# First group's shift and scale from row tiles of the conditioning weights, summed on DVE; tokens scaled on ACT

## Chip, cores, metric

One Trainium2 chip, one of its cores. The metric is the device time of one execution of the whole kernel in microseconds (us), as a median over runs. The engines are named as in the profile: PE is TensorE (PEld its weight loads), DVE is VectorE, ACT is ScalarE, POOL is GpSimd, SP is SyncE, which issues nearly all DMAs. MB are 10^6 bytes.

## The reference

One layer of a decoder trunk over 2048 tokens of width 1024 in float32. Only its beginning matters here: six vectors of 1024 values come from a conditioning vector c and a weight matrix, and the first two shift and scale the normalised tokens ahead of one wide projection.

```python
cond = jax.nn.silu(c)
mod = cond @ ada_w[l] + ada_b[l]                 # ada_w: 1024 x 6144
shift_m, scale_m, gate_m, shift_f, scale_f, gate_f = jnp.split(mod[:, None, :], N_MOD, axis=-1)
h = rms_norm(x, mix_norm_g[l]) * (1 + scale_m) + shift_m
proj = h @ w_in[l] + b_in[l]
...
x = x + gate_m * mixed
...
return rms_norm(x, final_norm_g)
```

Attention, a gated linear recurrence (HGRN2), an output projection and a gated feed-forward layer with a short convolution follow.

## The kernel before

Tokens are worked on in four groups of 512 (four blocks of 128 tokens). Channels stand in eight tiles of 128, index `k`. For each group the tokens are normalised, transposed with channels on the partitions, shifted and scaled, and split into a high part rounded to fp32r and a low part, the rest. Weights are split in the same way, and every product is three matmuls (high by high, high by low, low by high) that add up in one PSUM bank: `mm3`.

The first group has a stage of its own, in which everything is held in the written order on each engine (`pin(True, ...)` to `pin(False, ...)`, by `keep_in_program_order`); instructions that are not held are put into the engines' queues by the planner of the tile framework, the setup's mask tiles (`lvt`, `lev`) and other constants among them. The stage computes five projections of 128 columns (`first_cols`) for 512 tokens, with the loop over `k` outside, so that each of the eight steps needs shift and scale of 128 channels only: `first_mm(k, i)` is one `mm3` of step `k` into bank `ps0[i]`. That makes 8 x 5 x 3 = 120 matmuls of 128x512.

What a step needs, by name:

- `load_ada0(t)` loads one column tile of `ada_w`, all 1024 rows by 128 columns (0.5 MB, as 128 partitions x 8 rows of 512 B). Tiles 8 to 15 give the scale of channel tile `k`, tiles 0 to 7 its shift. Twelve buffers. SP issues them in written order with the loads of x, of the projection weights (`load_w0(kh)`, five loads for each half of the channels) and of later constants (`rB`).
- `first_mod(k)` multiplies a tile by `cond` (one instruction of 128x1024) and adds its eight parts in halves (512, 256, 128 columns). The scale tile is always DVE's; the shift tile is TensorE's for k = 0, DVE's for k = 1 and GpSimd's for k = 2 to 7 (`SHIFT`).
- `first_ab(k)` sums over the partitions with matmuls of one column into `mod_ps`; its `end()` adds biases on ACT and leaves shift and scale in `abm`.
- `norm_x` squares a token block on ACT, DVE adds the two halves, GpSimd makes the reciprocal root; `scale_x` multiplies the tokens by it, on DVE.
- `turn_x(k)` transposes four blocks on TensorE into the one bank `tp`; `first_h(k)` applies `abm` on ACT (tile `hf_h`), rounds the high part on ACT (`hhi`), and DVE subtracts for the low part (`hlo`).
- `split_w0(kh, ...)` splits the five weight tiles of one half: high parts on ACT (`w0h`), low parts (`w0l`) on DVE, in the first half two of five on GpSimd.

Step `k` hands the work of step `k + 1` to the queues ahead of its own products, and the sums of step `k + 3`. Behind the stage follow the other projections, HGRN2 and attention of group 0, then the other groups; the remaining 32 column tiles of `ada_w` are summed there, by `mod_part`, and are not touched.

Of the kernel before, what the change touches and what calls it, by code (L numbers as in the profile page):

```python
# [8 lines left out]
F32 = mybir.dt.float32  # L9
# [3 lines left out]
AF = mybir.ActivationFunctionType  # L13
ALU = mybir.AluOpType
# [4 lines left out]
P = 128  # L19
D = 1024  # L20
KT = D // P
KH = KT // 2
# [31 lines left out]
def kernel(ctx, tc, x, c, ada_w, ada_b, mix_norm_g, w_in, b_in, attn_sinks, attn_out_g,  # L54
# [32 lines left out]
    def bank(name, tag):  # L87
        return psp.tile([P, 512], F32, tag=tag, bufs=BANKS[tag], name=name)
# [43 lines left out]
    def col(nm, i=0, n=1):  # L132
        o = names[nm] + i
        return cols[:, o:o + n]
# [1 line left out]
    modc = const.tile([P, 48], F32, name="modc")  # L136
    abm = const.tile([P, 4, KT], F32, name="abm")

    def mod_sums(eng, raw, ns, times=True):

        if times:
            eng.tensor_tensor(out=raw, in0=raw, in1=cond.unsqueeze(2).broadcast_to([P, KT, P]), op=ALU.mult)
        for n in ns:
            eng.tensor_tensor(out=raw[:, 0:n, :], in0=raw[:, 0:n, :], in1=raw[:, n:2 * n, :], op=ALU.add)

    def mod_col(ps, raw, n, by=None):
        for k in range(n):
            TE.matmul(ps, lhsT=raw[:, k, :], rhs=ones[:, 0:1] if by is None else by[:, k:k + 1], start=k == 0,
                      stop=k == n - 1)

    def mod_ab(slot, gname, shift0, scale0, k0, n):
        ks_ = slice(k0, k0 + n)
        V.scalar_tensor_tensor(out=abm[:, slot, ks_], in0=modc[:, scale0 + k0:scale0 + k0 + n], scalar=1.0,
# [76 lines left out]
    with ExitStack() as mx:  # L230
# [18 lines left out]
        V.tensor_tensor(out=cond, in0=psC[:, 0:KT], in1=cond, op=ALU.mult)  # L249


        xs, xi = [], [None]
        ada0 = {}

        def load_x(b):
            if b < BPG:
# [10 lines left out]
                SY.dma_start(out=hs[i], in_=x_v[b * P:(b + 1) * P, i * 512:(i + 1) * 512])  # L267
            return hs

        def load_ada0(t):  # L270
            ada0[t] = su.tile([P, KT, P], F32, tag="ada0", bufs=12, name=f"ada0_{t}")
            SY.dma_start(out=ada0[t], in_=ada_v[:, :, t * P:(t + 1) * P])

        xs.append(load_x(0))
        load_ada0(8)
        xs.append(load_x(1))
        load_ada0(0)
        xs.append(load_x(2))
        xs.append(load_x(3))
        psA = bank("rowsA", "tp")  # L280
        TE.transpose(psA[:, 0:nA], rA[0:nA, :], ident[0:nA, 0:nA])
        V.tensor_copy(out=cols[:, 0:nA], in_=psA[:, 0:nA])
# [4 lines left out]
        def norm_x(t, b):  # L287
            r = norm_rows(su if b < BPG else mt, t, f"x{b}", "ln", 3)
            if b < BPG:
                return r  # L290
            for half in t:
                V.tensor_scalar(out=half, in0=half, scalar1=r, scalar2=None, op0=ALU.mult)
# [89 lines left out]
        ps0 = [bank(f"ps0_{i}", t) for i, t in zip(range(len(first_cols)), ("mm", "mm", "mm", "hg", "hg", "at"))]  # L382
        mod_ps = bank("mod_ps", "at")
        tps = {}
        SHIFT = [TE, V, G, G, G, G, G, G]

        def first_mod(k):
            for t in (KT + k, k):
                if t not in ada0:
                    load_ada0(t)  # L390
            mod_sums(V, ada0[KT + k], (4, 2, 1))
            if SHIFT[k] is not TE:
                mod_sums(SHIFT[k], ada0[k], (4, 2))

        def first_ab(k):

            ps = mod_ps[:, 2 * k:2 * k + 2]
            mod_col(ps[:, 0:1], ada0[KT + k], 1)
            if SHIFT[k] is TE:
                mod_col(ps[:, 1:2], ada0[k], KT, cond)  # L400
            else:
                mod_col(ps[:, 1:2], ada0[k], 2)

            def end():
                S.activation(abm[:, 0, k:k + 1], ps[:, 0:1], AF.Identity, scale=col("mix_g", k), bias=abg[:, k:k + 1])
                S.activation(abm[:, 1, k:k + 1], ps[:, 1:2], AF.Identity, bias=col("ada_b", k))
            return end

        def turn_x(k):
            tps[k] = bank(f"tp0_{k}", "tp")  # L410
            for b in range(BPG):
                TE.transpose(tps[k][:, b * P:(b + 1) * P], xs[b][k // 4][:, k % 4 * P:(k % 4 + 1) * P], ident)

# [7 lines left out]

        def scale_x(b, r):
            for half in xs[b]:
                V.tensor_scalar(out=half, in0=half, scalar1=r, scalar2=None, op0=ALU.mult)

        r = norm_x(xs[0], 0)
        mod_sums(V, ada0[KT], (4,))
        scale_x(0, r)
        r = norm_x(xs[1], 1)
        mod_sums(V, ada0[KT], (2, 1), False)  # L430
        scale_x(1, r)
        load_w0(0)
        ab0 = first_ab(0)
        r = norm_x(xs[2], 2)
        scale_x(2, r)
        r = norm_x(xs[3], 3)
        ab0()
        scale_x(3, r)
        turn_x(0)
        split_w0(0, (V, G))  # L440
        first_h(0)
        first_mod(1)
        turn_x(1)
        first_mm(0, 0)
        first_mm(0, 1)
        if SHIFT[1] is TE:
            first_ab(1)()
        for i in range(2, len(first_cols)):
            first_mm(0, i)
        if SHIFT[1] is not TE:  # L450
            first_ab(1)()
        first_mod(2)
        first_h(1)
        first_mod(3)
        load_w0(1)
        for k in range(1, KT):
            pos = [0,0,0,0,0,0,0,0][k]
            for i in range(len(first_cols)):
                if i == pos and k + 1 < KT:
                    turn_x(k + 1)  # L460
                    first_ab(k + 1)()
                    first_h(k + 1)
                    if k + 3 < KT:
                        first_mod(k + 3)
                if k == 2 and i == 2:
                    split_w0(1, (V, V))
                first_mm(k, i)
            if k == 5:
# [1116 lines left out]
```

## Time and profile before

| | |
|---|---|
| time, median of 3 runs | 2443.85 us (2443.26 to 2449.54) |
| the profiled execution | 2448.34 us, its span 2446.3 us |
| mean granted TensorE clock | 0.975 of full |
| PE busy | 2294.8 us, 94% |
| DVE busy | 1912.5 us, 78% |
| ACT busy | 966.7 us, 40% |
| POOL busy | 931.7 us, 38% |
| end of the first group's five projections | last of 120 matmuls starts at 80.94 us |

The busy times are those of the whole span, and say little about one stage: the first 81 us are 3% of it. For a stage the profile is asked for stretches of time (busy time of each engine between two times), for the timeline (instructions in order of time, equal neighbours merged) and for the waits (which engine sat idle, and whose signal ended it). A matmul's printed duration overlaps its neighbour's; the distance between two starts is what one takes. Line L46 is the helper that issues every instruction, so instructions are told apart by their tiles.

### The profile page before, as it was taken

The numbers are of one execution on the slowest core, as the hardware profiler recorded it, in microseconds if no ns is written. First come the engines' busy times: TensorE is split into PE (matmuls) and PEld (weight loads), VectorE is DVE, ScalarE is ACT, GpSimd is POOL, SyncE is SP. The second block draws the span as 40 slices with busy tenths as digits, with TensorE's granted clock in tenths as the row PEclk, the third lists the DMA queues.
The fourth block names the chain that finished last, engine by engine and source line by source line (L and its number), as shares of the span: only waits on it lengthen the run. The fifth ranks groups of instructions, "written<-read, shape, count | busy, mean of one in ns | idle before, by whom it ended". The sixth has DMA issues, their size and how long they took to land. (4 is left out here: it accounts for less than half of the span.)

```text
span 2446.3 us, 31473 instructions
## 1 busy us (share of the span) xinstructions
PE 2294.8 (94%) x11521; PEld 1904.1 (78%) x11521; DVE 1912.5 (78%) x2737; ACT 966.7 (40%) x1658; POOL 931.7 (38%) x776
## 2 busy tenths in 40 slices
PE   5889898998999899999999999999999989998997
PEld 4877787887788787887888888778888768786775
DVE  8888768788867877378888888878878688777666
ACT  3336523723552363455333333433333343233322
POOL 6222212213122222032756666478888721110101
PEclk8999999999999999999999999999999989999999
DMA  8342323323231238475434433554555488887543
GB/s 216 91 121 91 91 69 105 95 70 112 79 95 53 86 113 267 157 248 155 146 97 144 151 117 114 191 176 156 163 153 166 138 267 248 215 209 239 182 171 124
DMA packets 335445, 359.74 MB, mean 147 GB/s; under 512 B 12405, under 2 KB 279371, under 8 KB 335291
## 3 DMA queue, kind: packets, MB, share of 16 engines
q1 hardware_dynamic: 320315, 301.36, 39.3%
q0 software_dynamic: 14976, 56.37, 8.5%
q8 instruction: 91, 1.49, 0.2%
q14 instruction: 63, 0.52, 0.1%
HBM read 250.19 MB, written 107.49 MB: 146 GB/s over the span
## 5 line engine op out<-in xcount | busy, mean ns | idle before, releaser
L46 DVE SCALAR_TENSOR_TENSOR cc<-ub,cols,cc 128x1024 f32<-128x1024 f32 x88 | 153.2, 1741 | 15.5 <-ACT cc L46 13.3
L46 PE MATMUL lv<-a_q,K 128*128 128x128 f32 (+2 forms) x768 | 80.5, 265 | 42.7 <-DVE K L46 38.2
L46 ACT ACTIVATE Th<-da 128x896 fp32r<-128x896 f32 x88 | 81.8, 945 | 92.6 <-PE ps_d L46 88.2
L46 PEld LDWEIGHTS lv<-a_q,K 128*128 128x128 f32 (+2 forms) x768 | 72.2, 177 | 55.6 <-DVE K L46 28.8
L46 POOL DMA_DIRECT2D x_d<-o x32 | 27.2, 858 | 218.6 <-DVE o L46 218.6
L46 DVE TENSOR_TENSOR o<-ps_d,u 128x512 f32<-128x512 f32 x72 | 49.5, 687 | 71.6 <-ACT u L46 34.8
L46 DVE TENSOR_TENSOR Tl<-da,Th 128x896 fp32r<-128x896 f32 x88 | 94.5, 1099 | 12.8 <-ACT Th L46 12.8
L46 POOL TENSOR_TENSOR s<-wu_0r,s 128x512 f32<-128x512 f32 x44 | 59.2, 1347 | 107.2 <-DVE ws_0l L46 14.6
L46 DVE TENSOR_TENSOR cc<-cc,v 128x1024 f32<-128x1024 f32 x44 | 64.2, 1459 | 43.5 <-ACT cc L46 43.4
L46 POOL MEMSET AT<- 128x512 f32 x16 | 8.5, 533 | 234.8 <-PE ho L46 211.8
L46 POOL TENSOR_TENSOR s<-wu_1r 128x512 f32<-128x512 f32 x44 | 70.0, 1590 | 70.7 <-DVE t_T4l L46 16.2
L46 POOL TENSOR_TENSOR wu_1r<-wu_0r,wu_1r 128x512 f32<-128x512 f32 x44 | 93.3, 2121 | 3.1
L46 ACT ACTIVATE cc<-cc 128x1024 f32<-128x1024 f32 x44 | 46.7, 1061 | 120.8 <-DVE cc L46 120.8
L46 POOL TENSOR_SCALAR rv_d<-ssd 128x1 f32<-128x1 f32 x16 | 14.8, 925 | 181.6 <-ACT dx L46 181.6
L46 POOL TENSOR_TENSOR pl<-raw,ph 128x512 fp32r<-128x512 f32 x32 | 44.3, 1388 | 99.3 <-ACT ph L46 83.6
L46 POOL TENSOR_TENSOR s<-s,wu_0r 128x512 f32<-128x512 f32 x44 | 73.6, 1672 | 0.0
L46 DVE TENSOR_TENSOR v<-ps_u,v 128x512 f32<-128x512 f32 x88 | 60.4, 686 | 15.2 <-PE ps_u L46 11.9
L46 DVE COPY_PREDICATED AT<-lev,lv 128x512 f32<-128x512 uint32 (+1 forms) x96 | 70.1, 731 | 2.4 <-PE lv L46 1.1
L46 ACT ACTIVATE cc<-ub,cols 128x1024 f32<-128x1024 f32 x44 | 54.6, 1240 | 25.9 <-DVE ub L46 25.9
L46 DVE TENSOR_TENSOR ada<-ada,cond 128x1024 f32<-128x1024 f32 (+1 forms) x37 | 52.3, 1414 | 14.3 <-DMA ada<-in_ada_w_dram 14.3
L46 DVE TENSOR_TENSOR a_q<-a_q,tot 128x256 f32<-128x256 f32 x96 | 52.1, 543 | 12.4 <-PE lv L46 11.1
L46 DVE TENSOR_TENSOR ada<-ada 128x512 f32<-128x512 f32 (+3 forms) x82 | 61.2, 747 | 0.9
(2114 smaller groups left out, 8562.9 us busy)
## 6 DMA issues: line engine op xcount, KB each, us to landing
da<-act_d SPq DMA_DIRECT2D x88, 448.0 KB, 8.0
wu_0r<-in_w_up_dram SPq DMA_DIRECT2D x44, 512.0 KB, 4.6
wu_1r<-in_w_up_dram SPq DMA_DIRECT2D x44, 512.0 KB, 4.3
act_d<-cc POOLq DMA_DIRECT2D x42, 512.0 KB, 4.1
ada<-in_ada_w_dram SPq DMA_DIRECT2D x40, 512.0 KB, 6.0
x_d<-o POOLq DMA_DIRECT2D x32, 512.0 KB, 7.9
act_d<-sm POOLq DMA_DIRECT2D x21, 768.0 KB, 4.2
x<-in_x_dram SPq DMA_DIRECT2D x26, 512.0 KB, 5.6
```

The lines of the kernel that those rows point to most:

```text
L46: ins = fn(*args, **kwargs)
```

## The change

Shift and scale of the first group are computed for half of the channels at a time (`half`, four channel tiles), not for one tile. `load_ada0(half, k)` loads a row tile: 128 rows of `ada_w`, 512 columns of shift and 512 of scale (0.5 MB, 128 partitions x 2 rows of 2 KB); there are ten buffers. `first_mod(half, k)` adds it, times its column of `cond`, to a running sum in one DVE instruction of 128x1024 (for k = 0 a multiplication alone). After eight of them `first_ab(half)` makes eight one-column matmuls and three small DVE operations. GpSimd makes no sums and no low parts of weights. `scale_x` is on ACT. All eight tiles of the first half are asked for among the loads of x, ahead of the projection weights; those of the second half behind the first weights, the last two of them behind the second weights. Transposes have a second bank in turn, the tag `at`, and are issued a step earlier. The sums of the second half stand in steps 0 to 2, `split_w0(1)` at the start of step 3 and `first_ab(1)` behind two of its five products.

```diff
--- before.py
+++ after.py
@@ -136,18 +136,6 @@
     modc = const.tile([P, 48], F32, name="modc")
     abm = const.tile([P, 4, KT], F32, name="abm")
 
-    def mod_sums(eng, raw, ns, times=True):
-
-        if times:
-            eng.tensor_tensor(out=raw, in0=raw, in1=cond.unsqueeze(2).broadcast_to([P, KT, P]), op=ALU.mult)
-        for n in ns:
-            eng.tensor_tensor(out=raw[:, 0:n, :], in0=raw[:, 0:n, :], in1=raw[:, n:2 * n, :], op=ALU.add)
-
-    def mod_col(ps, raw, n, by=None):
-        for k in range(n):
-            TE.matmul(ps, lhsT=raw[:, k, :], rhs=ones[:, 0:1] if by is None else by[:, k:k + 1], start=k == 0,
-                      stop=k == n - 1)
-
     def mod_ab(slot, gname, shift0, scale0, k0, n):
         ks_ = slice(k0, k0 + n)
         V.scalar_tensor_tensor(out=abm[:, slot, ks_], in0=modc[:, scale0 + k0:scale0 + k0 + n], scalar=1.0,
@@ -249,8 +237,9 @@
...
         xs, xi = [], [None]
-        ada0 = {}
+        ada0, ada_sum = {}, {}
 
         def load_x(b):
             if b < BPG:
@@ -267,16 +256,27 @@
                 SY.dma_start(out=hs[i], in_=x_v[b * P:(b + 1) * P, i * 512:(i + 1) * 512])
             return hs
 
-        def load_ada0(t):
-            ada0[t] = su.tile([P, KT, P], F32, tag="ada0", bufs=12, name=f"ada0_{t}")
-            SY.dma_start(out=ada0[t], in_=ada_v[:, :, t * P:(t + 1) * P])
+        def load_ada0(half, k):
+
+            r = ada0[half, k] = su.tile([P, 2, 512], F32, tag="ada0", bufs=10, name=f"ada0_{half}_{k}")
+            SY.dma_start(out=r, in_=ada_v[:, k, 0:2 * D].rearrange("p (s c) -> p s c", s=2)
+                         [:, :, half * 512:(half + 1) * 512])
+
+        def first_mod(half, k):
+            raw = ada0.pop((half, k))
+            if k == 0:
+                ada_sum[half] = su.tile([P, 2, 512], F32, tag="adas", bufs=2, name=f"adas_{half}")
+                V.tensor_scalar(out=ada_sum[half], in0=raw, scalar1=cond[:, 0:1], scalar2=None, op0=ALU.mult)
+            else:
+                V.scalar_tensor_tensor(out=ada_sum[half], in0=raw, scalar=cond[:, k:k + 1], in1=ada_sum[half],
+                                       op0=ALU.mult, op1=ALU.add)
 
         xs.append(load_x(0))
-        load_ada0(8)
         xs.append(load_x(1))
-        load_ada0(0)
-        xs.append(load_x(2))
-        xs.append(load_x(3))
+        for k in range(KT):
+            load_ada0(0, k)
+            if k in (1, 2):
+                xs.append(load_x(k + 1))
         psA = bank("rowsA", "tp")
         TE.transpose(psA[:, 0:nA], rA[0:nA, :], ident[0:nA, 0:nA])
         V.tensor_copy(out=cols[:, 0:nA], in_=psA[:, 0:nA])
@@ -382,32 +382,21 @@
         ps0 = [bank(f"ps0_{i}", t) for i, t in zip(range(len(first_cols)), ("mm", "mm", "mm", "hg", "hg", "at"))]
         mod_ps = bank("mod_ps", "at")
         tps = {}
-        SHIFT = [TE, V, G, G, G, G, G, G]
-
-        def first_mod(k):
-            for t in (KT + k, k):
-                if t not in ada0:
-                    load_ada0(t)
-            mod_sums(V, ada0[KT + k], (4, 2, 1))
-            if SHIFT[k] is not TE:
-                mod_sums(SHIFT[k], ada0[k], (4, 2))
-
-        def first_ab(k):
-
-            ps = mod_ps[:, 2 * k:2 * k + 2]
-            mod_col(ps[:, 0:1], ada0[KT + k], 1)
-            if SHIFT[k] is TE:
-                mod_col(ps[:, 1:2], ada0[k], KT, cond)
-            else:
-                mod_col(ps[:, 1:2], ada0[k], 2)
-
-            def end():
-                S.activation(abm[:, 0, k:k + 1], ps[:, 0:1], AF.Identity, scale=col("mix_g", k), bias=abg[:, k:k + 1])
-                S.activation(abm[:, 1, k:k + 1], ps[:, 1:2], AF.Identity, bias=col("ada_b", k))
-            return end
+
+        def first_ab(half):
+
+            ps = mod_ps[:, 8 * half:8 * half + 8]
+            for i in range(2):
+                for kk in range(KH):
+                    TE.matmul(ps[:, 4 * i + kk:4 * i + kk + 1], lhsT=ada_sum[half][:, i, kk * P:(kk + 1) * P],
+                              rhs=ones[:, 0:1], start=True, stop=True)
+            ks_ = slice(KH * half, KH * half + KH)
+            V.tensor_tensor(out=abm[:, 0, ks_], in0=ps[:, 4:8], in1=col("mix_g", KH * half, KH), op=ALU.mult)
+            V.tensor_tensor(out=abm[:, 0, ks_], in0=abm[:, 0, ks_], in1=abg[:, ks_], op=ALU.add)
+            V.tensor_tensor(out=abm[:, 1, ks_], in0=ps[:, 0:4], in1=col("ada_b", KH * half, KH), op=ALU.add)
 
         def turn_x(k):
-            tps[k] = bank(f"tp0_{k}", "tp")
+            tps[k] = bank(f"tp0_{k}", "at" if k % 2 else "tp")
             for b in range(BPG):
                 TE.transpose(tps[k][:, b * P:(b + 1) * P], xs[b][k // 4][:, k % 4 * P:(k % 4 + 1) * P], ident)
 
@@ -421,48 +410,43 @@
 
         def scale_x(b, r):
             for half in xs[b]:
-                V.tensor_scalar(out=half, in0=half, scalar1=r, scalar2=None, op0=ALU.mult)
-
-        r = norm_x(xs[0], 0)
-        mod_sums(V, ada0[KT], (4,))
-        scale_x(0, r)
-        r = norm_x(xs[1], 1)
-        mod_sums(V, ada0[KT], (2, 1), False)
-        scale_x(1, r)
+                S.activation(half, half, AF.Copy, scale=r)
+
+        r0 = norm_x(xs[0], 0)
+        r1 = norm_x(xs[1], 1)
+        scale_x(0, r0)
+        first_mod(0, 0)
+        first_mod(0, 1)
+        r2 = norm_x(xs[2], 2)
+        scale_x(1, r1)
+        first_mod(0, 2)
+        r3 = norm_x(xs[3], 3)
+        scale_x(2, r2)
+        scale_x(3, r3)
+        turn_x(0)
+        turn_x(1)
         load_w0(0)
-        ab0 = first_ab(0)
-        r = norm_x(xs[2], 2)
-        scale_x(2, r)
-        r = norm_x(xs[3], 3)
-        ab0()
-        scale_x(3, r)
-        turn_x(0)
-        split_w0(0, (V, G))
+        for k in range(3, KT):
+            first_mod(0, k)
+        for k in range(6):
+            load_ada0(1, k)
+        load_w0(1)
+        for k in range(6, KT):
+            load_ada0(1, k)
+        first_ab(0)
         first_h(0)
-        first_mod(1)
-        turn_x(1)
-        first_mm(0, 0)
-        first_mm(0, 1)
-        if SHIFT[1] is TE:
-            first_ab(1)()
-        for i in range(2, len(first_cols)):
-            first_mm(0, i)
-        if SHIFT[1] is not TE:
-            first_ab(1)()
-        first_mod(2)
-        first_h(1)
-        first_mod(3)
-        load_w0(1)
-        for k in range(1, KT):
-            pos = [0,0,0,0,0,0,0,0][k]
+        split_w0(0, (V, V))
+        for k in range(KT):
             for i in range(len(first_cols)):
-                if i == pos and k + 1 < KT:
-                    turn_x(k + 1)
-                    first_ab(k + 1)()
+                if k == 3 and i == 2:
+                    first_ab(1)
+                if k + 1 < KT and i == (2 if k == 3 else 0):
                     first_h(k + 1)
-                    if k + 3 < KT:
-                        first_mod(k + 3)
-                if k == 2 and i == 2:
+                    if k + 2 < KT:
+                        turn_x(k + 2)
+                if k < 3 and i in (1, 2, 3) and 3 * k + i < 9:
+                    first_mod(1, 3 * k + i - 1)
+                if k == 3 and i == 0:
                     split_w0(1, (V, V))
                 first_mm(k, i)
             if k == 5:
```

## Rows read from the trace of the kernel before

**Rows 1.** Stretches: us, engines' busy us (instructions), TensorE clock, DMA share, GB/s.

```profile
0.00:20.00 20.00, 6.22 (x26) 5.28 (x27) 12.00 (x38) 11.16 (x28) 7.89 (x18) 1.00 0.93 273
20.00:44.00 24.00, 9.46 (x30) 6.84 (x28) 23.86 (x31) 2.13 (x5) 16.87 (x12) 0.76 1.14 279
44.00:65.00 21.00, 19.16 (x82) 15.76 (x83) 20.69 (x22) 8.40 (x18) 13.33 (x8) 0.79 0.28 76
65.00:81.40 16.40, 16.34 (x81) 13.13 (x80) 12.35 (x26) 11.56 (x19) 0.69 (x2) 1.00 0.60 184
```

**Rows 2.** Timeline, TensorE: start us, us, line, operation, tiles, count [idle before <-releaser].

```profile
12.20 3.55 PE L46 MATMUL mod_ps<-cond,ada 128*128 128x1 f32 x16
...
24.24 0.79 PE L46 MATMUL ps<-hlo,w0h 128*128 128x512 f32 x1 [3.09 <-DVE hlo L46]
...
29.33 0.39 PE L46 MATMUL ps<-hlo,w0h 128*128 128x512 f32 x1
...
50.77 0.60 PE L46 MATMUL tp<-ident,x 128*128 128x128 f32 x4
...
54.09 0.39 PE L46 MATMUL ps<-hhi,w0h 128*128 128x512 f32 x1
54.32 0.40 PE L46 MATMUL ps<-hlo,w0h 128*128 128x512 f32 x1
...
57.92 0.83 PE L46 MATMUL mod_ps<-ones,ada 128*128 128x1 f32 x6 [1.83 <-DVE ada L46]
...
59.89 0.63 PE L46 MATMUL ps<-hhi,w0l 128*128 128x512 f32 x1
60.31 0.63 PE L46 MATMUL ps<-hhi,w0h 128*128 128x512 f32 x1
...
80.94 0.40 PE L46 MATMUL ps<-hhi,w0l 128*128 128x512 f32 x1
```

**Rows 3.** Waits until 82 us: who waited for whom, us, times, longest.

```profile
ACT abm L46 <- PE mod_ps L46: 38.1, 8, 16.9
```

**Rows 4.** Stretches of the ada tile alone: us, busy us of each engine, clock, DMA.

```profile
20.00:45.00 25.00, 2.48 (x11) 2.31 (x12) 13.04 (x12) 17.74 (x11) 0.75 1.10 268
...
60.00:81.40 21.40, 2.18 (x18) 2.25 (x18) 6.30 (x11) 0.00 (x0) 0.92 0.55 165
```

**Rows 5.** Timeline, DVE: start us, us, tiles, one addition of 128x512.

```profile
25.44 2.38 DVE L46 TENSOR_TENSOR ada<-ada 128x512 f32<-128x512 f32 x1
```

**Rows 6.** Tile hf_h until 90 us: count, ns min/median/max, first to last start.

```profile
L46 ACT ACTIVATE hf_h<-tp,abm x8: 772/778/783, 18.8 to 74.7; 128x512 f32<-128x512 f32 x8
L46 ACT ACTIVATE hhi<-hf_h x8: 630/632/633, 19.6 to 75.5; 128x512 fp32r<-128x512 f32 x8
L46 DVE TENSOR_TENSOR hlo<-hf_h,hhi x8: 678/683/694, 23.5 to 76.2; 128x512 fp32r<-128x512 f32 x8
```

**Rows 7.** Tile lvt, the setup's masks, until 90 us, same columns.

```profile
L46 DVE SCALAR_TENSOR_TENSOR lvt<-fx,up_s x5: 280/292/1980, 14.2 to 37.1; 128x128 f32<-128x128 f32 x5
```

**Rows 8.** Tile cc, a later stage of the kernel, same columns.

```profile
L46 DVE SCALAR_TENSOR_TENSOR cc<-ub,cols,cc x88: 1271/1694/2301, 1142.5 to 1977.9; 128x1024 f32<-128x1024 f32 x88
```

**Rows 9.** Stretches, DMA: us, TensorE clock, DMA share, GB/s.

```profile
0.00:5.00 5.00, 1.00 0.35 104
5.00:10.00 5.00, 1.00 1.09 333
10.00:12.00 2.00, 1.00 1.05 400
20.00:28.00 8.00, 1.00 1.21 291
64.00:66.00 2.00, 1.00 1.08 381
```

**Rows 10.** Timeline, ACT: the first square of the second token block.

```profile
9.50 0.63 ACT L46 ACTIVATE junk_x<-x 128x512 f32<-128x512 f32 x1 [2.20 <-DMA x<-in_x_dram]
```

**Rows 11.** Timeline, DVE: one small operation of eight columns.

```profile
4.22 0.16 DVE L46 SCALAR_TENSOR_TENSOR abg<-cols 128x8 f32<-128x8 f32 x1
```

## Prediction

> **What bounds the kernel now.** I read the stretches of the first 81 us before anything else, because the diff touches only the work up to the end of the first group's five projections. [rows 1] show a stage that is not held by TensorE: its 120 products need 120 x 0.234 = 28 us at the high clock, 2.4 GHz (spacing in [rows 2]: 54.09 to 54.32), yet the last one starts at 80.94. In 20 to 44 us DVE is busy 23.9 of 24 and GpSimd 16.9, in 44 to 65 DVE 20.7 of 21; only after 65, with GpSimd at 0.7, is TensorE busy throughout. DMA carries 279 GB/s until 44 us and then has almost nothing to do (76 GB/s). So DVE sets the pace from 20 to 65 us, beside a DMA stream for the first half of that time.
>
> The view of waits says for whom that matters: ACT waits 38.1 us in eight waits for the sums that give it shift and scale [rows 3]. The stretches of the ada tile alone show DVE's share: 13.0 us in 12 instructions while GpSimd does 17.7 us on its own ada tiles, and 6.3 us in 11 when GpSimd does none [rows 4]. One instruction shows the same: a 128x512 addition takes 2.38 us at 25.44 [rows 5]; the same shape with two inputs takes 0.68 where GpSimd is idle (the low part in [rows 6], its shortest). A 128x128 mask operation goes from 0.28 to 1.98 us [rows 7]. GpSimd's sums and DVE's hold each other up.
>
> **The change, part by part.**
>
> *Sums.* Removed: fifteen of the sixteen 0.5 MB column tiles with a multiplication and two or three additions each, six on GpSimd (the sixteenth is multiplied on TensorE). Added: sixteen row tiles, one 128x1024 instruction each on DVE. The shortest three-operand instruction of that shape takes 1.27 us [rows 8]; the longest there, 2.30, has GpSimd beside it, and there is no such neighbour now. I take 1.27, so 8 x 1.27 = 10.2 us per half, against the DVE-and-GpSimd work of [rows 4], 33 us of DVE alone over the stage.
>
> *DMA.* The bytes are the same, but rows of 512 B become rows of 2 KB. 512 B rows run at 291 GB/s (20 to 28 us), a stretch of 1 KB rows at 381 (64 to 66), and one that holds mostly 4 KB rows at 400 (10 to 12) [rows 9]. No row shows 2 KB alone, so the bounds are 291 and 400; I take 370, next to the 1 KB row. The Trainium skill (DMA: Bandwidth & Descriptors, section Where 436 GB/s comes from) puts the HBM side of one core at about 358 GB/s. By that the first half would land 0.5 us later; the 381 of the row speaks against a cap there, and the sum does without it.
>
> The order is changed too: x and all eight tiles of the first half come before the projection weights, the second half behind those. By 5 us 0.52 MB have arrived [rows 9]. x1 needed 1.6 MB, which the 333 GB/s of 5 to 10 us deliver at 8.3; ACT started on it at 9.50 [rows 10], so a tile is usable 1.2 to 1.3 us after its bytes by rate. The last tile of half 0 ends 6.34 MB: 5 + 5.82/0.37 = 20.7, usable 22.0. The first half of the weights (1.31 MB, 512 B rows still) is usable from about 23 to 26.5; ACT comes to it at 27, so its place behind the tiles costs nothing. The second half of ada and of the weights ends at 25.2 + 4.19/0.37 + 1.31/0.291 = 41.0, usable 42.2. Ten buffers stand for sixteen loads: load 11 waits for sum 1 (done about 11 us), load 16 for sum 6 (about 20), before SP reaches them. The small loads of later constants stay behind it on SP and are not needed until the seventh step.
>
> *First product.* Sum 7 of half 0 ends at 22.0 + 1.3 = 23.3. Eight 128x1 products: 16 took 3.55 us, soon after TensorE's start [rows 2], so 1.8; three small DVE operations 3 x 0.16 [rows 11]; ACT h 0.78, ACT high part 0.63 [rows 6], first weight split another 0.63; 27.7, with handovers 28.0. Before, products run from 24.24 [rows 2]: this later start is the price of the change. ACT scaling x instead of DVE: eight operations of at most 0.63, done by 20, under the arrival of the tiles. DVE's weight low parts (0.68 each, five, no longer shared with GpSimd) keep ahead of three products at 1.28.
>
> *Loop.* TensorE resumes at the low clock, 1.2 GHz (spacing 0.42, as from 59.89 to 60.31): from 24.24 it took until 29.33 for the spacing to halve [rows 2]. I count ten products of step 0 at 0.427 and five at 0.234: 5.4, to 33.4. Steps 1 and 2 are 15 x 0.234 + 0.6 for four transposes [rows 2] = 4.1 each, to 41.6, and two projections of step 3 to 43.0. DVE in that time: low parts and the second half's sums, the last of them after its tile, 42.2 + 1.3 = 43.5; here the DMA is late next, TensorE waits 0.5. Then column products 0.9 (high clock), but DVE has the five weight low parts of the second half ahead of the three small operations: 43.5 + 5 x 0.68 + 0.5 = 47.4, ACT h 48.2, high part 48.8, low part 49.5. TensorE has the rest of step 3 and four transposes until 47.2, so it waits 1.6 us plus 0.5 within step 4. Step 4 ends at 49.5 + 14 x 0.234 = 52.8, step 5 with transposes 56.9, step 6 60.4, step 7 with the constants' transpose 64.2. Before, the last product starts at 80.94 and ends the stage at 81.2. Saved: 17.0.
>
> *Corrections.* (a) The masks: sixteen DVE operations of the setup that are not held in written order stand inside this stage, 0.28 us apiece [rows 7], 4 us in all. If all lay between the last sum and the first product they cost 4, if all lay before, 0. DVE needs some 12 of the first 23 us, so I take 1. (b) A TensorE wait of 2 us before 57.92 was followed by products 0.42 apart again from 59.89 [rows 2]; if that lasts as long as after 24.24, 5 us, it is at most twelve products at +0.19 = 2.3. The two waits above are 0.5 and 2.1 us: between 0 and 2.3, I take 1. Net 15.0.
>
> What follows (HGRN and attention of group 0) starts from these projections and from DVE's queue, not at a time of its own, so I carry the gain through. Against the profiled execution, 2448.34 (span 2446.3, 2.0 around it): 2433.3. That execution is 4.5 above the median of the runs, so against 2443.85 I forecast 2429.
>
> **Rivals.**
>
> 1. *The stream stays at 291 GB/s.* For: that is what this tensor has shown [rows 9]; against: those were 512 B rows. The first half is then usable at 5 + 20.0 + 1.3 = 26.3, the first product at 32.3, the last tile at 49.0, step 4's low part, from 50.3 by the chain above, at 56.3, the stage's end at 71. Saved 10, less the corrections 2: 2436.
>
> 2. *The later plan takes most of it up.* What is not held in order is placed by a planner, and the new stage gives it other gaps. For: masks of the setup already stand among the sums [rows 7]. Against: the stages behind it depend on data of this one. From 11 us lost on it the gain is under 4: about 2441.
>
> 3. *TensorE never comes up to the high clock* and the change is slower. [rows 1] have it at 0.76 and 0.79 of full over 45 us of this stage, and [rows 2] show the fall after one pause. If all 120 products keep 0.427: 28.0 + 51.2 + six sets of transposes at 1.2 + 1.8 = 88.2, 7.0 later than now: 2451, with the waits hidden. It decides from about 90 low products of 120 (15.0 / 0.193 = 78 beyond the ten counted). Against: before 54 us the spacing was at 0.234 again although DVE still starved it, and the new loop has two pauses in all. The Trainium skill (TensorE: Matmul & The Clock Gate, section HAM oscillation — how this bites in real kernels) tells of just this: loops whose waits between bursts of products put the engine back to the low rate each time. By it pauses are what to fear in a start from cold; the trace agrees that one pause of 2 us was enough [rows 2].
>
> That the change does not do what it says is not a rival of weight: the sums, tiles and bytes are written out and leave no choice to the planner.
>
> **How the numbers follow.** Forecast (2423 to 2433): 0.66. Better than that, with neither correction and rates near 400, 2418 to 2423: 0.05. Rival 1, 2433 to 2438: 0.13, of which 0.12 under the bound below. Rival 2: 0.11. Rival 3: 0.05. A measurement of this kernel tells 0.3%, 7.3 us, from no change, so faster means under 2436.5: 0.66 + 0.05 + 0.12 = 0.83. Within 0.3%: 0.01 + 0.11 = 0.12. Slower: 0.05. The range 2419 to 2438 takes in the forecast, rival 1 and most of the better case, 0.8 of the chance.
>
> **What would show it.** Right: no ada work on GpSimd; sixteen DVE instructions near 1.3 us; DMA above 350 GB/s while row tiles load; first products at about 28, full spacing from about 33; a pause of TensorE of 1 to 3 us before step 4; last of the first 120 products at about 64; the work behind shifted by the same 15 us. Wrong, if: DVE's sums run at 1.7 or more; products keep 0.427 past step 1; the last tile lands near 49; or the stage ends near 64 and the total does not follow.

## The result

The kernel after takes 2431.42 us (median of 5 runs), the kernel before beside it 2445.52 (5 runs): a ratio of 0.9936, 95% interval 0.9920 to 0.9952. That is 14.1 us less; the forecast was 2429 against a median of 2443.85, 15 less. Two further sets of runs of the same two kernels gave 0.9934 (0.9922 to 0.9946) and 0.9933 (0.9918 to 0.9949). One of the five runs of after was slow, with a granted clock of 0.749 and 2848.68 us; the ratio is taken without it, and the median of the other four is 2430.77, 14.8 us less than before. The profiled execution of after took 2433.72 us, its span 2431.9.

The stretches of after, in the columns of [rows 1]:

```profile
20.00:44.00 24.00, 18.89 (x80) 15.14 (x79) 18.25 (x23) 10.73 (x18) 0.00 (x0) 1.00 0.90 286
44.00:65.00 21.00, 19.96 (x98) 15.93 (x98) 13.41 (x32) 11.74 (x16) 0.80 (x2) 1.00 0.72 213
```

Against [rows 1], GpSimd has 0.8 us of work from 20 to 65 us, DVE has slack from 20 us on (18.3 of 24, 13.4 of 21), and TensorE, which had 9.5 us of work in 20 to 44, now has 18.9. The clock of 1.00 in the first row has to be read with care: the trace holds no record of the clock before 31.4 us, and until then the products below are 0.43 us apart, which is the spacing of 1.2 GHz. From there to the end of the stage it is at 2.4 GHz in this execution.

TensorE's timeline, as in [rows 2]:

```profile
23.03 3.57 PE L46 MATMUL mod_ps<-ones,adas 128*128 128x1 f32 x16 [2.88 <-DVE adas L46]
...
29.18 0.79 PE L46 MATMUL ps<-hhi,w0h 128*128 128x512 f32 x1
...
31.47 0.39 PE L46 MATMUL ps<-hhi,w0l 128*128 128x512 f32 x1
...
44.18 1.95 PE L46 MATMUL mod_ps<-ones,adas 128*128 128x1 f32 x16 [0.95 <-DVE adas L46]
...
49.06 0.49 PE L46 MATMUL ps<-hhi,w0h 128*128 128x512 f32 x1
49.79 0.50 PE L46 MATMUL ps<-hlo,w0h 128*128 128x512 f32 x1 [0.23 <-DVE hlo L46]
...
63.97 0.40 PE L46 MATMUL ps<-hhi,w0l 128*128 128x512 f32 x1
```

The one-column products of the first half run at 23.03, the first real product at 29.18, some five products later, at 31.47, they are at the spacing of the high clock, the second half's one-column products stand at 44.18 behind a wait on DVE, step 4 starts at 49.06, and the last of the 120 products at 63.97, where it was 80.94 in [rows 2]: 17.0 us earlier.

The sums (tile adas, columns as in [rows 8]), and the place in DVE's timeline where they set the pace:

```profile
L46 DVE SCALAR_TENSOR_TENSOR adas<-ada,cond,adas x14: 1276/1284/1286, 10.0 to 42.8; 128x1024 f32<-128x1024 f32 x14
```

```profile
16.00 0.15 DVE L46 TENSOR_TENSOR ss_x<-ss_x 128x1 f32<-128x1 f32 x1
...
16.33 1.28 DVE L46 SCALAR_TENSOR_TENSOR adas<-ada,cond,adas 128x1024 f32<-128x1024 f32 x1
...
19.06 3.92 DVE L46 SCALAR_TENSOR_TENSOR adas<-ada,cond,adas 128x1024 f32<-128x1024 f32 x3
```

Sixteen instructions do what 53 did on two engines, at 1.28 us, the shortest of [rows 8], not its middle one of 1.69. From 16.33 us they follow each other without a wait for a tile (the last three merge into one row of 3.92 us).

The DMA stream, as in [rows 9]:

```profile
0.00:5.00 5.00, 1.00 0.35 96
5.00:12.00 7.00, 1.00 1.04 401
12.00:16.00 4.00, 1.00 1.03 392
16.00:20.00 4.00, 1.00 1.04 383
20.00:24.00 4.00, 1.00 1.18 300
```

Rows of 2 KB run at 383 GB/s (16 to 20 us), and at 392 where a quarter of the bytes are still x with its rows of 4 KB (12 to 16); the stretch with 512 B rows of the projection weights (20 to 24) at 300.

Is the 17 us all there at the end? I paired each instruction of after with the one that has the same place in its engine's order before, and took the difference of the starts. Behind the stage TensorE and SP have the very order of before. The difference is -17.2 us at 180 to 240 us, -18.1 at 600, -17.9 at 1500, -14.9 at 1620 and -14.3 at the end. So the gain is carried through 1500 us, and 3.0 us of it go in one place, where both kernels pass from one half of the feed-forward stage to the next. TensorE's waits show the two steps. The first 1.0 us goes at 1533 to 1536, in two waits of 0.33 and 0.75 us for low parts whose source came later by DMA; most of the rest goes here, first after, then before:

```profile
1566.25 1.29 POOL L46 TENSOR_TENSOR s<-wu_1r 128x512 f32<-128x512 f32 x1 [8.68 <-DMA wu_1r<-in_w_up_dram]
1592.64 0.51 PE L46 MATMUL ps_u<-t_T3h,wvs_3h 128*128 128x512 f32 x1 [0.94 <-ACT wvs_3h L46]
```

```profile
1579.92 1.60 POOL L46 TENSOR_TENSOR s<-wu_1r 128x512 f32<-128x512 f32 x1 [5.46 <-DMA wu_1r<-in_w_up_dram]
1608.09 0.40 PE L46 MATMUL ps_u<-t_T3h,wvs_3h 128*128 128x512 f32 x1
```

The weight tile `wu_1r` was asked for 16.9 us earlier after (1556.70, not 1573.58) and used by GpSimd only 13.7 earlier: from issue to use the load took 3.2 us longer. GpSimd, ACT and DVE pass that on, and TensorE waits where it did not wait before. The clock has a small part at most: it was low for longer in after at that place (0.57 of full from 1546 to 1554, against 0.79 before), which cost 0.65 us, and a wait of 0.44 that only before had took most of that back. Why the load took longer is open. It belongs to this execution: in two more executions of after, told of below, the same place costs 0.4 and 0.7 us.

### The profile page after: what moved, and what is told of

It reads as the page before. It is cut to its first block, busy times and chain, and to the rows that moved or that the text cites. A ratio compares the mean times of both kernels' runs of the same rounds, so it can differ in the third digit from the quotient of the medians.

```text
span 2431.9 us, 31366 instructions
## 1 busy us (share of the span) xinstructions
PE 2285.8 (94%) x11493; PEld 1896.8 (78%) x11493; DVE 1883.3 (77%) x2718; ACT 967.1 (40%) x1650; POOL 897.0 (37%) x756
## 5 line engine op out<-in xcount | busy, mean ns | idle before, releaser
L46 DVE TENSOR_TENSOR o<-ps_d,u 128x512 f32<-128x512 f32 x72 | 49.5, 687 | 70.8 <-ACT u L46 34.8
L46 DVE TENSOR_TENSOR cc<-cc,v 128x1024 f32<-128x1024 f32 x44 | 63.1, 1434 | 43.5 <-ACT cc L46 43.4
L46 POOL TENSOR_SCALAR rv_d<-ssd 128x1 f32<-128x1 f32 x16 | 14.8, 924 | 180.8 <-ACT dx L46 180.8
L46 DVE TENSOR_TENSOR ub<-ps_u,u 128x512 f32<-128x512 f32 x88 | 60.0, 681 | 0.1
L46 DVE TENSOR_TENSOR o<-o,dgate 128x1024 f32<-128x1024 f32 x48 | 57.1, 1216 | 0.0
```

The source lines that it names most:

```text
L46: ins = fn(*args, **kwargs)
```

## Experiments

**GpSimd's sums put on DVE, in the kernel before** (b_allv).

```diff
-        SHIFT = [TE, V, G, G, G, G, G, G]
+        SHIFT = [TE, V, V, V, V, V, V, V]
```

> The kernel before, with the six shift sums of GpSimd put on DVE; nothing else is touched. Theory A: GpSimd's sums bought nothing, since they stretched DVE's by as much as they took off it. A scale tile on DVE alone goes by in 2.3 us (1.13 + 0.60 + 0.34 + 0.20 between starts after 64 us), a shift tile in 2.1, so 8 x 2.3 + 7 x 2.1 = 33 us, which is what DVE already spends on ada tiles before. By A the last of the 120 products starts at 75 to 83 us (80.94 before) and the total stays within 6 us of before. Theory B: GpSimd was a real helper, and the gain of the change comes from fewer instructions and faster rows alone. By B six shift tiles of 2.1 us more on the engine that sets the pace end the stage 10 to 13 us later, near 92, and the total is above 2452.

Measured: 0.9964 of before (0.9951 to 0.9977), 2441.43 us against 2449.26 in that set. The last product, and a stretch of the ada tile (columns as in [rows 4], without GpSimd, which has no ada work here):

```profile
73.06 0.40 PE L46 MATMUL ps<-hhi,w0l 128*128 128x512 f32 x1
```

```profile
20.00:45.00 25.00, 2.84 (x18) 2.90 (x18) 18.72 (x27) 0.86 1.10 269
```

DVE does 18.7 us of ada work in 27 instructions where [rows 4] show 13.0 in 12, 0.69 us apiece in place of 1.08. The mask operations that took up to 1.98 us in [rows 7] do not exceed 0.29.

Theory A holds and was too modest: the help of GpSimd did not come out even, it cost 7.9 us of the stage (80.94 to 73.06), and the total is 7.8 lower where A had it within 6. The clock is not behind it: in both traces 27 products of the stage are at the spacing of 1.2 GHz. Theory B, 10 to 13 us later, is out.

**GpSimd kept busy, in the kernel after** (a_gpbusy).

```diff
+        idle = su.tile([P, KT, P], F32, name="idle")
+        G.memset(idle, 1.0)
+        for n in range(6):
+            G.tensor_tensor(out=idle, in0=idle, in1=cond.unsqueeze(2).broadcast_to([P, KT, P]), op=ALU.mult)
+            for m in (4, 2):
+                G.tensor_tensor(out=idle[:, 0:m, :], in0=idle[:, 0:m, :], in1=idle[:, m:2 * m, :], op=ALU.add)
```

> The kernel after, with work of the old size put back on GpSimd on a tile that nobody reads: six multiplications of 128x1024 and six pairs of additions, about 26 us from 18 us on; the row tiles have nine buffers, not ten, to make room. Theory A (the two engines hold each other up): the sums on DVE beside it go from 1.28 us to 1.7 or more, the low parts from 0.68 to over 1, and the last product starts at 69 to 74 us, not 63.97; the total rises by 5 to 10 us. Theory B (DVE was slow before only through its many instructions): sums stay at 1.3, the stage ends by 65, the total stays within 2 us of after.

Measured: 0.9992 of before (0.9982 to 1.0003): the gain is gone, some 14 us where A had 5 to 10. The sums, the start of the second half's one-column products (44.18 after) and the last product:

```profile
L46 DVE SCALAR_TENSOR_TENSOR adas<-ada,cond,adas x14: 1275/1285/2916, 10.5 to 57.1; 128x1024 f32<-128x1024 f32 x14
L46 DVE TENSOR_SCALAR adas<-ada,cond x2: 754/1268/1781, 8.8 to 43.0; 128x1024 f32<-128x1024 f32 x2
```

```profile
58.42 1.95 PE L46 MATMUL mod_ps<-ones,adas 128*128 128x1 f32 x16 [0.95 <-DVE adas L46]
...
78.21 0.40 PE L46 MATMUL ps<-hhi,w0l 128*128 128x512 f32 x1
```

The longest sum takes 2.92 us and the multiplication up to 1.78 where it took 0.75; the mean of the fourteen sums is 1.65, a little under what A named, and the low parts average 1.12. The stage ends 14.2 us later than after, where A had 5 to 10. TensorE's waits for DVE show where: 5.74 us ahead of the first half's one-column products (2.88 in after) and 3.69 ahead of the low part at 50.98 us, while the products are still those of the first half. No sum waits for its tile from 19.57 us on, so the tenth buffer, which had to make room here, is not the reason.

**Rows of 512 B** (a_rows512): the same tiles, each as eight pieces of 128 columns.

```diff
-            r = ada0[half, k] = su.tile([P, 2, 512], F32, tag="ada0", bufs=10, name=f"ada0_{half}_{k}")
-            SY.dma_start(out=r, in_=ada_v[:, k, 0:2 * D].rearrange("p (s c) -> p s c", s=2)
-                         [:, :, half * 512:(half + 1) * 512])
+            r = ada0[half, k] = su.tile([P, KT, P], F32, tag="ada0", bufs=10, name=f"ada0_{half}_{k}")
+            for s in range(2):
+                SY.dma_start(out=r.rearrange("p (q s) e -> p s q e", s=2)[:, s, :, :],
+                             in_=ada_v[:, k, s * D + half * 512:s * D + (half + 1) * 512]
+                             .rearrange("p (q e) -> p q e", q=KH))
```

> The kernel after, with the same bytes and the same DVE work, but rows of 512 B: each row tile is loaded in two halves into pieces of 128 columns. Theory A (the stream is just ahead of the sums, 0.6 us in the first half and 1.7 in the second, at 390 GB/s): at 291 GB/s the first half lands 3.7 us later and the second 7.4, so the first product starts near 32 us, the last at 69 to 70, and the total rises by 5 to 6 us. Theory B (DVE's sums bound the stage and the rows are worth nothing): the last product by 65.5.

Measured: 0.9943 (0.9929 to 0.9958), 2435.49 us. The stream, one of the sums, the first product, the second half's one-column products and the last product:

```profile
30.00:40.00 10.00, 1.00 1.21 291
```

```profile
23.16 1.28 DVE L46 SCALAR_TENSOR_TENSOR adas<-ada,cond,adas 128x1024 f32<-128x1024 f32 x1 [0.51 <-DMA ada<-in_ada_w_dram]
```

```profile
32.46 0.79 PE L46 MATMUL ps<-hhi,w0h 128*128 128x512 f32 x1
...
49.24 1.95 PE L46 MATMUL mod_ps<-ones,adas 128*128 128x1 f32 x16 [1.42 <-DVE adas L46]
...
69.93 0.40 PE L46 MATMUL ps<-hhi,w0l 128*128 128x512 f32 x1
```

The stream is back at 291 to 298 GB/s from 20 us on, DVE waits 0.40 to 0.53 us for each of the last three tiles of the first half, which it never does in that place after, and the stage ends at 69.93, within A. That is 6.0 us later than after in its first profile. The second half's one-column products start 5.1 us later (44.18 after); the rest came behind them, where the clock was low again from 51 to 55 us. In the total, where A had 5 to 6 us, nothing is shown: the ratio lies 0.0007 to 0.0010 above those of after, some 2 us, and the intervals overlap.

**Tokens scaled on DVE** (a_scalev).

```diff
-                S.activation(half, half, AF.Copy, scale=r)
+                V.tensor_scalar(out=half, in0=half, scalar1=r, scalar2=None, op0=ALU.mult)
```

> The kernel after, with the tokens scaled on DVE again, not on ACT: eight instructions of 0.45 us between starts. Theory A (DVE's queue sets the start of the first product, since its last five sums run back to back from 16.3 us): the first product starts 1.5 to 3.5 us later (29.18 after), the last by as much, the total rises by 1.5 to 3.5 us. Theory B (DVE waits for tiles anyway): both within 0.5 us of after.

Measured: 0.9943 (0.9928 to 0.9958), 2435.53 us. First and last product:

```profile
31.46 0.79 PE L46 MATMUL ps<-hhi,w0h 128*128 128x512 f32 x1
...
66.26 0.39 PE L46 MATMUL ps<-hhi,w0l 128*128 128x512 f32 x1
```

Both are 2.3 us later than after in its first profile, as A has it, and 1.6 to 1.8 later for the first product than in the two further executions of after (29.68 and 29.91): DVE's queue sets the start of the first product, and moving the scaling to ACT is worth 1.6 to 2.3 us there. In the total, where A had 1.5 to 3.5, it cannot be told from noise: the interval holds all three ratios of after.

**Two instructions a tile** (a_twoops).

```diff
-                V.scalar_tensor_tensor(out=ada_sum[half], in0=raw, scalar=cond[:, k:k + 1], in1=ada_sum[half],
-                                       op0=ALU.mult, op1=ALU.add)
+                V.tensor_scalar(out=raw, in0=raw, scalar1=cond[:, k:k + 1], scalar2=None, op0=ALU.mult)
+                V.tensor_tensor(out=ada_sum[half], in0=raw, in1=ada_sum[half], op=ALU.add)
```

> The kernel after, with each row tile multiplied in place and then added, two DVE instructions of 128x1024 in place of one. Theory A (the single multiply-add is a part of the gain of its own, since DVE's sums run back to back at the end of both halves): 0.70 + 1.15 us between starts in place of 1.32, so the last five sums of the first half end about 3 us later and those of the second 7 to 8 us; first product near 32 us, last at 70 to 73, total 6 to 9 us over after. Theory B (the stream sets the pace): last product by 66.

Measured: 0.9973 (0.9962 to 0.9984), 2442.14 us, beside 2434.15 for after in the same set. The instructions; the first product, the second half's one-column products and the last product; and a stretch of TensorE (us, busy time, granted clock, DMA share, GB/s):

```profile
L46 DVE TENSOR_SCALAR ada<-ada,cond x14: 745/747/753, 10.4 to 50.2; 128x1024 f32<-128x1024 f32 x14
L46 DVE TENSOR_TENSOR adas<-ada,adas x14: 1217/1222/1226, 11.3 to 51.0; 128x1024 f32<-128x1024 f32 x14
```

```profile
32.79 0.79 PE L46 MATMUL ps<-hhi,w0h 128*128 128x512 f32 x1
...
52.26 3.57 PE L46 MATMUL mod_ps<-ones,adas 128*128 128x1 f32 x16 [2.40 <-DVE adas L46]
...
75.08 0.40 PE L46 MATMUL ps<-hhi,w0l 128*128 128x512 f32 x1
```

```profile
50.00:60.00 10.00, 7.74 (x28) 0.50 0.63 194
```

The first product starts as forecast. The one-column products of the second half start 8.1 us later than the 44.18 of after, near the 7 to 8 of A; the last product is 11.1 us later, 2 over A's upper end, and the 3.0 us in between go with the clock, which was at 1.2 GHz from 50 to 60 us. The total is 8.0 us over after in the same set, as A has it. The single multiply-add carries more of the gain than either the rows or the scaling.

**The kernel after again, twice** (a_again, a_third).

> The kernel after, unchanged, beside the three others of this set, as their measure: last product at 64.0 us, total 14 to 16 us under before.

> The kernel after, unchanged, once more beside the two others of this set, as their measure: last product at 64 to 65.4 us, by the phase of the clock at its start; total 14 to 17 us under before.

Measured: 2434.28 and 2434.15 us, 16.4 and 14.3 under before in their sets. But the last product stood at 65.35 and at 67.22, not at 63.97. Steps 0 to 3 start within 1.2 us of each other; the difference is made after TensorE's wait for the second half's sums. Stretches of TensorE there (us, busy time, granted clock, DMA share, GB/s), a_again and then a_third, and the last product of a_third:

```profile
46.00:48.00 2.00, 2.00 (x13) 0.74 0.77 202
48.00:50.00 2.00, 2.00 (x6) 0.50 1.02 353
```

```profile
46.00:48.00 2.00, 2.00 (x11) 0.50 0.61 155
48.00:50.00 2.00, 2.00 (x7) 0.50 1.10 378
50.00:52.00 2.00, 2.00 (x6) 0.50 0.68 190
```

```profile
67.22 0.40 PE L46 MATMUL ps<-hhi,w0l 128*128 128x512 f32 x1
```

The pause was 0.31 and 0.89 us (0.95 in the first profile, where the clock held), and 2 to 2.7 us of one-column products followed it each time. Behind them one execution ran 3.4 us at 1.2 GHz, the other from 46 to nearly 53 us (0.81 of full in 52 to 54). Which of the two, the pause or the one-column products, makes the clock fall was not tried apart. In a_scalev, where the one-column products follow the others without a pause, it did not fall.

**TensorE kept busy at the start** (a_warm).

```diff
+        def turn_more(n):
+            for _ in range(n):
+                TE.transpose(ps0[4][:, 0:P], ident, ident)
...
+                if k == 0 and b == 2:
+                    turn_more(14)
...
         turn_x(1)
+        turn_more(14)
...
         first_ab(0)
+        turn_more(14)
         first_h(0)
```

> The kernel after, with 42 transposes of the identity added on TensorE, into a bank whose first real product clears it: 14 between the third and fourth token block, 14 ahead of the one-column products, 14 behind them. No other engine's work is touched. Theory A (the start is paid at the low clock): the sixteen passes of one-column products take 2.0 us instead of 3.57, the first products 0.234 instead of 0.427, the last product starts at 61.0 to 62.5 (63.97), the total falls by 1.5 to 3 us. Theory B (their wait is on DVE and ACT, and TensorE has room): last product at 63.5 or later, no change beyond 1 us.

Measured: 0.9932 (0.9919 to 0.9945), 2433.71 us beside 2434.28 for after.

```profile
23.20 1.95 PE L46 MATMUL mod_ps<-ones,adas 128*128 128x1 f32 x16 [1.82 <-DVE adas L46]
...
28.00 0.78 PE L46 MATMUL ps<-hhi,w0h 128*128 128x512 f32 x1
...
62.71 0.40 PE L46 MATMUL ps<-hhi,w0l 128*128 128x512 f32 x1
```

The one-column products take 1.95 us in place of 3.57, the first product starts at 28.00, the last at 62.71: 1.3 us before the best of after, 0.2 past the late end of A and ahead of B's 63.5. The other part of A did not come: the first two products are still 0.43 to 0.57 us apart, since the clock, raised by the added transposes, fell again behind TensorE's wait of 1.82 us and the one-column products that followed it:

```profile
26.00:28.00 2.00, 2.00 (x12) 0.50 1.06 390
```

In the total, where A had 1.5 to 3 us, it does not show (0.6).

**Transposes and the small operations ahead** (a_tuned): as a_warm, with the low parts of two of five weight tiles put behind `first_ab(1)`.

```diff
-                    split_w0(1, (V, V))
+                    split_w0(1, (V, V), range(3))
...
                     first_ab(1)
+                    split_w0(1, (V, V), range(3, 5))
```

> The kernel with added transposes, and the last two low parts of the second half of the weights put behind the three small operations of the second half's shift and scale. Theory A (step 4 waits for DVE's five low parts ahead of these three): step 4 starts 0.9 us earlier than with the transposes alone, the last product at 60.5 to 62.0 us; the total 2 to 3.5 us under after. Theory B (what a stage wins by one or two us does not show behind the changes of the clock from one execution to the next): the stage as by A, the total within 1.5 us of after.

Measured: 0.9930 (0.9917 to 0.9942), 2431.72 us beside 2434.15 for after.

```profile
47.26 0.69 DVE L46 TENSOR_TENSOR hlo<-hf_h,hhi 128x512 fp32r<-128x512 f32 x1 [0.29 <-ACT hhi L46]
```

DVE did its part: the three small operations begin as soon as the one-column products end, and the low part of step 4 begins at 47.26, against 49.04 in after and 47.78 with the transposes alone, so 0.5 us of it is due to the new place of the two low parts. But the clock was at 0.50 of full from 46 to 48 us in this execution, so the last product stands at 63.97 all the same, outside A. The 2.4 us under after lie inside the two kernels' intervals; I call it no more than not slower.

**Quarters** (a_quarter; a_quarter_warm with the added transposes): row tiles of 2 x 256 columns, 32 sums of 128x512. The edit in its main lines:

```diff
-            r = ada0[half, k] = su.tile([P, 2, 512], F32, tag="ada0", bufs=10, ...)
+            r = ada0[half, k] = su.tile([P, 2, 256], F32, tag="ada0", bufs=20, ...)
...
+                if odd_k and p < 4 and i == 2:
+                    first_ab(p)
...
+                if not odd_k and p < 4 and i < 4:
+                    first_mod(p, 2 * i)
+                    first_mod(p, 2 * i + 1)
```

> The kernel after with the halves cut into quarters: row tiles of two channel tiles, 0.26 MB with rows of 1 KB, 32 DVE instructions of 128x512, four one-column products a quarter; the second half of the projection weights comes ahead of the third quarter, its split at step 1. Theory A (the price of the change is the late first product, since nothing starts before 4.2 MB and eight sums are through; behind it TensorE needs 4 us a step): the first quarter ends at 4.2 MB of the stream and is usable near 16 us, the first product at 20 to 23 us, the last at 54 to 58, the total 6 to 10 us under after. Theory B (smaller tiles cost what they win: 1 KB rows and 256 KB transfers run slower, DVE pays more per element): last product at 62 or later, total within 2 us of after.

> The quarters with the 28 added transposes ahead of the first one-column products and 14 behind them. Theory A: the last product 1.5 to 3 us before that of the quarters alone, the total lower by as much. Theory B (the added transposes stand in front of the one-column products, as the sums now come as early as the tokens): no gain, or a loss of up to 2 us.

Measured: 0.9950 (0.9935 to 0.9965) and 0.9951 (0.9939 to 0.9963): 4 to 5 us over after.

```profile
22.68 0.80 PE L46 MATMUL ps<-hhi,w0h 128*128 128x512 f32 x1
...
32.72 1.73 PE L46 MATMUL mod_ps<-ones,adas 128*128 128x1 f32 x8 [3.35 <-DVE adas L46]
...
70.08 0.40 PE L46 MATMUL ps<-hhi,w0l 128*128 128x512 f32 x1
```

```profile
26.68 0.48 DVE L46 TENSOR_SCALAR adas<-ada,cond 128x512 f32<-128x512 f32 x1
27.20 5.47 DVE L46 SCALAR_TENSOR_TENSOR adas<-ada,cond,adas 128x512 f32<-128x512 f32 x7
```

The first product starts at 22.68 as A forecast, 6.5 us ahead of after, and the last at 70.08, 6 us behind (69.77 with the added transposes, which gain 0.3 and not 1.5 to 3: there B holds). B had a part of the reason, that DVE pays more per element: eight sums of a quarter take 6.0 us (0.5 + 5.5), not half of the 10.0 of a half. It also had the slower stream: 1 KB rows by themselves run at 348 GB/s (32 to 40 us), though no sum waits for a tile here. Neither theory had the rest: the sums stand behind the low parts, so TensorE is through step 1 and waits 3.35 us for them at 32.72, and about 2 us again for the third and the fourth quarter. Here the early start was worth nothing, since the next piece was not ready; whether another order of DVE's queue would feed quarters was not tried.

## Why the prediction held, step by step

**What bound the kernel before: right.** DVE held the stage and GpSimd's help hurt. The forecast only said that the two hold each other up; b_allv gives the price, 7.9 us.

**Sums: right.** 1.28 us measured, 1.27 forecast.

**DMA: right in kind, 5% low.** 370 GB/s was taken for 2 KB rows, 383 to 392 came. The Trainium skill (DMA: Bandwidth & Descriptors, section Where 436 GB/s comes from) has about 358 GB/s for HBM to one core; the 383 to 392 of after lie above it, so here the measurement decides. The last tile of the first half was through by about 20 us (the sum of the rates shown), and the forecast had 20.7.

**First product: 28.0 forecast, 29.18 measured, and two terms were off.** The eight one-column products were counted as 1.8 us and took 3.57: the x16 of the row in [rows 2] are the matmuls of eight products, two for each, and I read them as sixteen products. The same slip made 0.9 of 1.95 in the second half. The other way went the sums: the last ended at 22.98 by queue, not at 23.3 by tile. I had DVE waiting for its last tile; it was held up earlier, behind the sum of squares of the fourth token block at 16.00, and then ran back to back. a_scalev shows that by adding to this queue. One reading was wrong as well: 24.24 is not the first product of before. One stands ahead of it, and TensorE then waits for the low part:

```profile
20.37 0.78 PE L46 MATMUL ps<-hhi,w0h 128*128 128x512 f32 x1
```

By the first product the later start, the price of the change, is 8.8 us and not the 4.9 between 24.24 and 29.18; the sum for after does not use it.

**Clock at the start: too cautious.** Ten products at the low clock were counted, some five came, and eight in a_again.

**Second half: 43.5 forecast for the last sum, 44.1 measured, but by DVE, not by the stream.** DVE's sums there run behind the low parts without a wait for a tile, so "the DMA is late next" was wrong; a_rows512 shows the case in which it is true, 69.93, and its working in the prediction (rival 1) said 71. (By the numbers that the rival names, its last tile comes at 49.7 and not 49.0, so 71.7.)

**Step 4: right for DVE and ACT.** The high part on ACT ended at 49.0 (48.8 forecast), the low part at 49.7 (49.5); the five low parts stood ahead of the three small operations. TensorE's pause in front of step 4 did not come: 1.6 + 0.5 us were forecast, 0.23 is in the trace (49.79), because the one-column products took a microsecond longer and left it work until then.

**End of the stage: 64.2 forecast, 63.97 measured.** The terms that were too small (2.8 us for the one-column products) and too large (stream, clock, TensorE's pause) cancel, so this agreement is luck in part.

**The total: 15.0 forecast, 14.3 in the profiled pair, and luck in part.** The stage gave 17.0 in this execution, as the working had it ahead of the corrections, and not 15.0; then 3.0 us went at 1533 to 1594 us, in a place that the forecast did not look at. In the other two executions the stage gave 15.6 and 13.7 and the end 13.8 and 10.0. Before was traced once, so how far its own stage moves from execution to execution is not known.

**Corrections.** The masks: all were done by 19.1 us, three of them, 0.8 us, between the last sums, and a row of others kept DVE from the sum of squares at 16.00 for up to 0.8 us after ACT had finished its part at 15.2; 1 was taken. The clock after a pause: 0 to 2.3 was the bound, 1 was taken; three profiles of after end the stage at 63.97, 65.35 and 67.22, about 0, 1.4 and 3.3 later than the first, so the bound was too low: I let a low stretch last no longer than after 24.24, and one lasted nearly seven microseconds. The rule that I set beside rival 3, from the Trainium skill (TensorE: Matmul & The Clock Gate, section HAM oscillation — how this bites in real kernels), tells of such waits between bursts of products. The traces of after agree in two executions of three: the low clock came back behind pauses of 0.31 and 0.89 us with one-column products behind them, and not behind one of 0.95.

**Rivals.** 1 did not come and was shown to be real by a_rows512. 2 did not come: TensorE's order behind the stage is the one of before, and the shift is carried. 3 did not come: products are at the spacing of 2.4 GHz from 31.5 us on in the first profile, and low for 3.4 and 6.8 us of the stage's second half in the other two.

What the gain consists of, by the experiments, each against the stage end of after in its first profile: GpSimd's work away 14.2 us, one instruction and not two 11.1, longer rows 6.0, scaling on ACT 2.3. The clock, with its up to 3.3 us between executions of one kernel, lies in each of these numbers. Taken at the start of the second half's one-column products, ahead of where those executions part (44.18, 44.67 and 44.91 in the three of after), they are 14.2, 8.1, 5.1 and 2.4. They overlap, since each alone makes another resource the last one, and do not add up to 17.0. The other parts of the change, the second bank for transposes, the order of the loads and DVE in place of ACT behind the one-column products, were not tried alone.

## What to carry to other kernels

Before giving an engine's spare time to the one beside it, look at how long the neighbour's instructions become: here DVE alone was 7.9 us faster than DVE with GpSimd's help. Choose the tile so that one instruction folds a whole transfer into a running sum, and let DMA rows grow with it. When counting a matmul's price from a merged row, divide by the products in the code and not by the x of the row.

## What had not been expected of the hardware

A float32 product with one column appears as two matmuls and two weight loads in the trace: 0.45 us for both at 1.2 GHz (3.57 us for eight in a_twoops, granted clock 0.50) and 0.24 at 2.4 (1.95 for eight in after, at 44.18).

Executions of one kernel differ by several us, in this stage through the clock: a pause of 0.3 to 0.95 us in the same place, with one-column products behind it, was followed by none, 3.4 or 6.8 us at 1.2 GHz. The stage's end moves by 3.3 us with that, and the profiled executions of after ended 14.3, 13.8 and 10.0 us ahead of the one of before, with 17.0, 15.6 and 13.7 at the end of the stage. A gain of 1 to 2 us at one place, as in a_warm and a_tuned, cannot be told from that.
